# New duration estimates for the scheduler that orders one encoder block's instructions

## The chip, the cores and the metric

The kernel runs on one core of a Trainium2 chip. Its engines are TensorE (PE; PEld is its loading of stationary operands), VectorE (DVE), ScalarE (ACT), GpSimd (POOL) and SyncE (SP, which here only issues transfers). Each engine takes its instructions strictly in the order in which the program holds them. The metric is the device time of one execution in microseconds, less being better.

## The reference

One layer of a streaming encoder, 512 tokens of width 1024, float32:

```python
mod = silu(c) @ w_ada + b_ada                   # six vectors of 1024
h   = rms(x, norm1_g) * (1 + sc1) + sh1
z   = h @ w_in                                   # split by columns into
rec = hgrn2(rq, rf, ri, rg)                      # 4 heads of a gated linear recurrence
att = dsa_attention(aq, ak, av, iq, ik, iw)      # 8 heads, 256 (or 128) keys chosen per row by an index score
x   = x + g1 * (concat(rec, att) @ w_out)
h2  = rms(x, norm2_g) * (1 + sc2) + sh2
x   = x + g2 * moe(h2)                           # 16 experts, two per token inside one of four groups
```

## The kernel before

All matrix products of float32 data are made from halves: a high part rounded to fp32r (`wh`, the high half of `hx` or `mix`) and the rest (`wl`), three products per pair. ScalarE rounds the high part, VectorE subtracts it to get the low one.

The work up to the experts is written as generators, one for a piece of work, that run under a small list scheduler, `Desk`, while the program is being built. Each instruction that a generator emits goes through `Engine.call`, which estimates its duration (`cost`) and books it on its engine; `Desk.run` always steps the generator that could start first by these estimates, with a rank as tie-break inside windows of 100 ns. So the table of estimates decides nothing but the order of the instructions on each engine, and, through `either`, whether some subtractions stand on VectorE or on GpSimd (POOL). The order of the expert loop is written out by hand.

The pieces of work that matter below:

- `norm1_gen` turns eight chunks of `w_ada` into the scale and shift of the first norm: a product `a<-chunk,cB`, a copy `row`, a product `a<-sel,row`, then VectorE's `gs` and `xt` and `hx_gen`, which makes the operand `hx[k]`.
- `z_gen` makes the 33 pieces of the input projection, 24 products each (`z<-hx,wh` and `z<-hx,wl`). The first four pieces run side by side (banks z, z, o and u) and take each `hx[k]` as it comes; the fourth is `u<-hx,wB`.
- `score_gen` and `topk_gen` are the index scores and the choice of the keys, `hgrn_gen`, `level_gen` and `end_gen` the recurrence. Its subtractions `dd<-b` (seven per head) go to VectorE or POOL by `either`.
- `attend_gen(j)`, `pair_gen` and `unit_gen` are attention for the j-th of four pairs of heads, in four blocks of rows. The bias of a pair, `Wb`, comes by a transfer that POOL issues; the last two blocks add a mask to it on POOL (`nl<-Wb,negm`). A unit is: bias sum on VectorE (`nl<-a,Wb`), exponential on ScalarE, transposition on PE, a copy (`PT`), and the product `u<-PT,vv`.
- `ada_gen` is the rest of `mod`: eight groups of eight steps on VectorE (`acc<-dd,cT`), each on a transfer of 256 KB; a group ends in products on PE (`a<-acc,ones` and `a<-cs,vc`), a copy on ScalarE and a transfer that POOL issues (`modD<-acc`).
- `out_gen` is the output projection (`z<-wh,mix`), its first half on the heads of the recurrence, its second on attention's.

What POOL issues stands in POOL's one order too: a transfer behind `modD<-acc` waits until that group's copy is done.

Of the kernel before, what the change touches and what calls it, by code (L numbers as in the profile page):

```python
# [9 lines left out]
F32 = mybir.dt.float32  # L10
F32R = mybir.dt.float32r
# [6 lines left out]
PSUM = bass.MemoryType.PSUM  # L18
DRAM = bass.MemoryType.DRAM

T, D, P = 512, 1024, 128
# [143 lines left out]
class Engine:  # L165
# [5 lines left out]
    def __getattr__(self, op):  # L171
        f = getattr(self.eng, op)
        if "dma" in op or op.startswith("preload"):
            return f

        def call(*a, **k):
            r = f(*a, **k)  # L177
            o = k["out"] if "out" in k else a[0]
            n = int(np.prod(o.shape[1:]))
            port = self.name == "pool"  # L180
            if self.name == "dve" and getattr(o, "space", None) != PSUM:
                ins = [x for x in [*a[1:], k.get("in0"), k.get("in1")]
                       if hasattr(x, "shape") and int(np.prod(x.shape[1:])) > 1 and getattr(x, "space", None) != PSUM]
                port = len(ins) > 1 or op in ("tensor_copy", "tensor_scalar") and len(ins) == 1
            if self.name == "pe":
                w = a[1]
                if op == "transpose":
                    cost = 107.0
                elif w.dtype == BF16:
                    cost = max(0.4167 * n, 28.0)  # L190
                elif o.shape[0] == 32:
                    cost = 0.4167 * n
                else:
                    cost = max(0.4167 * n * (4 if w.dtype == F32 else 1), 213.0 * w.shape[0] * o.shape[0] / P ** 2)
                    if w.dtype == F32R and w.shape[0] == 64:
                        cost /= 2
            else:
                rate = self.RATE[self.name]
                if op in ("max", "activation") or op.startswith("reduce"):
                    n = int(np.prod(a[1].shape[1:])) + 100 * ("accum_out" in k)  # L200
                if op.startswith("tensor_scalar") or op in ("memset", "tensor_copy"):
                    src = a[1] if op != "memset" else None
                    if self.name == "pool" or src is None or getattr(src, "space", None) != PSUM:
                        rate *= 0.52
                cost = 60 + n * rate
            self.desk.issue(self.name, cost, port)
            return r

        return call
# [1492 lines left out]
```

## Time and profile before

| | us |
|---|---|
| median of 3 runs (lowest, highest) | 728.02 (727.63, 729.42) |
| the profiled execution | 727.48 |
| its span, first to last instruction | 725.6 |

The span is 1.9 us shorter than the execution that holds it. Of the span, PE is busy 94%, VectorE 87%, ScalarE 61%, POOL 28%. A busy PE counts every matmul from its start to a modelled end, so gaps of a few tenths of a microsecond between products do not show there. The work under the scheduler takes the span's first 412 us or so, the expert loop the rest.

### The profile page before, as it was taken

Reading aid. Unit: us, or ns where it says so; the run is one execution under the profiler, and the core shown is the slowest. Engines: PE = TensorE matmul, PEld = TensorE weight load, DVE = VectorE, ACT = ScalarE, POOL = GpSimd, SP = SyncE. Lnnn points to the kernel's source line nnn. Section 1 sums busy time; section 2 is a strip of 40 time slices with the busy share of each in tenths; the row PEclk is TensorE's granted clock in tenths of the full one; section 3 lists DMA queues with packets and bytes.
Section 4 is the critical chain, followed back from the end, with each engine's and each line's share of the span. In section 5 each row is a group of like instructions: output and inputs, shape, how many; then the busy total and the mean of one; then the engine's idle time right before and its main releaser. Section 6 shows DMA issues by size and latency. Waiting matters only on the chain.

```text
span 725.6 us, 10941 instructions
## 1 busy us (share of the span) xinstructions
PE 683.1 (94%) x3794; PEld 530.9 (73%) x3794; DVE 630.9 (87%) x1057; ACT 439.0 (61%) x670; POOL 202.4 (28%) x104
## 2 busy tenths in 40 slices
PE   3999999999999999999889979999999999999993
PEld 1666778877778776667568858888888888888872
DVE  4637889999999987978866889999999999999991
ACT  4326664545557466553343458888777777777770
POOL 0120010001321321122200030165655655556412
PEclk9999999999999999999989999999999999999997
DMA  9947532231120324685697889999999999999502
GB/s 363 406 154 224 190 111 88 89 115 59 56 90 30 117 88 164 225 308 181 188 362 305 315 318 406 390 376 347 365 363 367 354 350 358 364 361 349 187 11 33
DMA packets 57388, 172.84 MB, mean 238 GB/s; under 512 B 11954, under 2 KB 12530, under 8 KB 56304
## 3 DMA queue, kind: packets, MB, share of 16 engines
q1 hardware_dynamic: 45168, 150.54, 56.1%
q0 software_dynamic: 10720, 17.24, 8.5%
q10 hardware_dynamic: 1440, 4.31, 1.5%
q8 instruction: 32, 0.52, 0.3%
q14 instruction: 28, 0.23, 0.1%
HBM read 167.50 MB, written 15.24 MB: 252 GB/s over the span
## 4 chain that ended last, share of the span: by engine, by line
PE 50%; DMA 21%; DVE 14%; issue 10%; ACT 3%; SPq 0%; POOL 0%; POOLq 0%; DVEq 0%; ACTq 0%
PE z L177 30%; PE a L177 14%; DMA w<-in_w_dram 13%; DVE wl L177 8%; DMA out_dram<-yo,idx 6%; PE u L177 2%; PE h L177 2%; PE o L177 2%; DMA dd<-in_w_ada_dram 1%; DMA chunk<-in_w_ada_dram 1%; DVE yo L177 1%; DVE xl L177 1%; DVE oh L177 1%; ACT wh L177 1%; ACT sq L177 1%
## 5 line engine op out<-in xcount | busy, mean ns | idle before, releaser
L177 ACT CAST wh<-w 128x1024 fp32r<-128x1024 f32 x168 | 174.5, 1054 | 44.2 <-PE h L177 30.9
L177 DVE TENSOR_TENSOR wl<-w,wh 128x1024 fp32r<-128x1024 f32 x168 | 196.6, 1216 | 2.4 <-ACT wh L177 2.0
L177 PE MATMUL z<-hx,wh 128*128 128x512 f32 x496 | 163.1, 409 | 1.1 <-DVE hx L177 0.6
L1358 POOL DMA_INDIRECT out_dram<-yo,idx x16 | 123.7, 7730 | 120.8 <-DVE wl L177 64.1
L177 PEld LDWEIGHTS z<-hx,wh 128*128 128x128 f32 x496 | 88.8, 189 | 27.1 <-issue 8.7
L177 PE MATMUL h<-wl,xh 128*128 128x512 f32 x256 | 101.4, 396 | 0.0
L177 PE MATMUL h<-wh,xh 128*128 128x512 f32 x256 | 100.8, 394 | 0.0
L177 PE MATMUL h<-wh,xl 128*128 128x512 f32 x256 | 100.6, 393 | 0.0
L177 ACT CAST wh<-raw 128x1024 fp32r<-128x1024 f32 x64 | 67.1, 1052 | 55.3 <-PE z L177 48.0
L177 PE MATMUL z<-hx,wl 128*128 128x512 f32 x248 | 97.6, 394 | 0.0
L177 DVE TENSOR_TENSOR wl<-raw,wh 128x1024 fp32r<-128x1024 f32 x64 | 81.6, 1286 | 6.8 <-ACT wh L177 6.5
L177 PEld LDWEIGHTS h<-wl,xh 128*128 128x128 f32 x256 | 48.5, 189 | 12.9 <-DVE wl L177 3.0
L177 PEld LDWEIGHTS h<-wh,xh 128*128 128x128 f32 x256 | 48.5, 189 | 10.2
L177 PEld LDWEIGHTS h<-wh,xl 128*128 128x128 f32 x256 | 48.4, 189 | 10.1 <-DVE xl L177 0.3
L177 PE MATMUL y<-wh,hh 128*128 128x512 f32 x128 | 53.0, 414 | 2.0 <-DVE yo L177 2.0
L177 PEld LDWEIGHTS z<-hx,wl 128*128 128x128 f32 x248 | 46.8, 189 | 10.3
L177 PE MATMUL y<-wl,hh 128*128 128x512 f32 x128 | 50.6, 396 | 0.0
L177 PE MATMUL y<-wh,hl 128*128 128x512 f32 x128 | 50.6, 395 | 0.0
L177 PE MATMUL z<-wh,mix 128*128 128x512 f32 x128 | 48.3, 421 | 0.0
L177 DVE SCALAR_TENSOR_TENSOR acc<-dd,cT,acc 128x512 f32<-128x512 f32 x56 | 43.8, 782 | 3.6 <-DMA dd<-in_w_ada_dram 3.0
L177 POOL TENSOR_TENSOR dd<-b 128x512 f32<-128x512 f32 (+1 forms) x14 | 17.2, 1242 | 93.5 <-PE a L177 79.0
L1353 POOL DMA_INDIRECT xe<-h2D,idx x15 | 17.1, 1140 | 80.5 <-DVE idx L177 46.3
(290 smaller groups left out, 1145.2 us busy)
## 6 DMA issues: line engine op xcount, KB each, us to landing
w<-in_w_dram SPq DMA_DIRECT2D x164, 512.0 KB
raw<-in_w_in_dram SPq DMA_DIRECT2D x33, 512.0 KB
dd<-in_w_ada_dram SPq DMA_DIRECT2D x64, 256.0 KB
raw<-in_w_dram SPq DMA_DIRECT2D x24, 512.0 KB
chunk<-in_w_ada_dram SPq DMA_DIRECT2D x8, 1024.0 KB
raw<-in_w_out_dram SPq DMA_DIRECT2D x8, 512.0 KB
lineR<-lineD POOLq DMA_DIRECT2D x4, 640.0 KB, 17.6
xt<-in_xT_dram SPq DMA_DIRECT2D x4, 512.0 KB
```

What stands on the lines that cost most here:

```text
L177: r = f(*a, **k)
L1353: pool.indirect_dma_start(out=dst, out_offset=None, in_=h2D, in_offset=bass.IndirectOffsetOnAxis(ap=ix, axis=0), bounds_check=T - 1, oob_i ...
L1358: pool.indirect_dma_start(out=out, out_offset=bass.IndirectOffsetOnAxis(ap=ix, axis=0), in_=y, in_offset=None, bounds_check=T - 1, oob_is_ ...
```

## The change

The formulas of `cost` get other numbers. On PE a float32 transposition goes from 107 to 110 ns, the fp32r product of 512 columns from 213 to 231 ns, the 32-row products get a base of 60 ns, float32 products 1.95 ns a column. ScalarE's instructions become 50 ns dearer when they read PSUM and 90 ns dearer otherwise, and an accumulated output counts as 220 instead of 100 elements. On VectorE and POOL, four kinds of instruction become 100 ns dearer.

```diff
                 if op == "transpose":
-                    cost = 107.0
+                    cost = 110.0
                 elif w.dtype == BF16:
-                    cost = max(0.4167 * n, 28.0)
+                    cost = max(0.4167 * n, 50.0)
                 elif o.shape[0] == 32:
-                    cost = 0.4167 * n
+                    cost = 60 + 0.3 * n
+                elif w.dtype == F32R:
+                    cost = 18 + 0.4167 * n
+                    if w.shape[0] == 64:
+                        cost = max(cost / 2, 70.0)
                 else:
-                    cost = max(0.4167 * n * (4 if w.dtype == F32 else 1), 213.0 * w.shape[0] * o.shape[0] / P ** 2)
-                    if w.dtype == F32R and w.shape[0] == 64:
-                        cost /= 2
+                    cost = max(1.95 * n, 225.0 * o.shape[0] / P)
...
-                    n = int(np.prod(a[1].shape[1:])) + 100 * ("accum_out" in k)
+                    n = int(np.prod(a[1].shape[1:])) + 220 * ("accum_out" in k)
...
                 cost = 60 + n * rate
+                if self.name == "act":
+                    cost += 50 if getattr(a[1], "space", None) == PSUM else 90
+                elif op in ("scalar_tensor_tensor", "tensor_tensor_reduce", "tensor_tensor_scan", "copy_predicated"):
+                    cost += 100
```

No instruction is added or removed; five change their engine. Four of the 14 `dd<-b` subtractions that stood on POOL and its one `mix<-sq,mix` now stand on VectorE.

What moves is shown at three places. The first is PE near the end of the first norm, from the product on the last chunk (`chunk_322` before, `chunk_319` after) on. The operands `hx_411` and `hx_442` before are `hx[6]` and `hx[7]`; after, these are `hx_403` and `hx_436`, and `hx_336` and `hx_375` are `hx[4]` and `hx[5]`. Before:

```order
L177 MATMUL a_413<-chunk_322,cB_102 32x256 x8
L177 MATMUL z_179<-hx_411,wh_165 128x512 x2
L177 MATMUL z_179<-hx_411,wl_166 128x512
L177 MATMUL z_214<-hx_411,wh_201 128x512 x2
L177 MATMUL z_214<-hx_411,wl_202 128x512
L177 MATMUL a_413<-sel4_104,row_423 128x1 x2
L177 MATMUL o_250<-hx_411,wh_233 128x512 x2
L177 MATMUL o_250<-hx_411,wl_234 128x512
L177 MATMUL u_294<-hx_411,wB_274 128x512 x2
L177 MATMUL u_294<-hx_411,wB_275 128x512
L177 MATMUL z_179<-hx_442,wh_165 128x512 x2
L177 MATMUL z_179<-hx_442,wl_166 128x512
```

And now:

```order
L177 MATMUL a_402<-chunk_319,cB_102 32x256 x8
L177 MATMUL z_179<-hx_403,wh_165 128x512 x2
L177 MATMUL z_179<-hx_403,wl_166 128x512
L177 MATMUL a_402<-sel4_104,row_417 128x1 x2
L177 MATMUL z_210<-hx_403,wh_197 128x512 x2
L177 MATMUL z_210<-hx_403,wl_198 128x512
L177 MATMUL o_254<-hx_403,wh_234 128x512 x2
L177 MATMUL o_254<-hx_403,wl_235 128x512
L177 MATMUL u_294<-hx_336,wB_274 128x512 x2
L177 MATMUL u_294<-hx_336,wB_275 128x512
L177 MATMUL u_294<-hx_375,wB_274 128x512 x2
L177 MATMUL u_294<-hx_375,wB_275 128x512
```

The fourth piece now lags two operands behind the others (three more of its products, on `hx[6]`, follow, then the products on `hx[7]`). Six products fewer stand ahead of the last chunk's product, nine fewer ahead of its `a<-sel,row`, and 15 instead of 6 between that one and the first product on `hx[7]`.

The second place is VectorE just ahead of the third pair's first bias sum (`ISA nl,nmx<-a,Wb 128x128`). Before:

```order
L177 TENSOR_SCALAR acc<-dd,cT 128x512
L177 SCALAR_TENSOR_TENSOR acc<-dd,cT,acc 128x512
L177 TENSOR_TENSOR mix<-sq,mix 128x512
L177 SCALAR_TENSOR_TENSOR acc<-dd,cT,acc 128x512
L177 TENSOR_TENSOR wl<-raw,wh 128x1024
L177 SCALAR_TENSOR_TENSOR acc<-dd,cT,acc 128x512
L177 TENSOR_TENSOR raw<-raw,g1b 128x1024
L177 SCALAR_TENSOR_TENSOR acc<-dd,cT,acc 128x512
L177 ISA nl,nmx<-a,Wb 128x128
```

And now:

```order
L177 TENSOR_SCALAR acc<-dd,cT 128x512
L177 SCALAR_TENSOR_TENSOR acc<-dd,cT,acc 128x512 x7
L177 SCALAR_TENSOR_TENSOR sq<-u,vc,sq 128x512
L177 TENSOR_TENSOR wl<-raw,wh 128x1024
L177 TENSOR_TENSOR mix<-sq,mix 128x512
L177 TENSOR_TENSOR raw<-raw,g1b 128x1024
L177 ISA nl,nmx<-a,Wb 128x128
```

The fourth group of `ada_gen` is now complete there; before, four of its eight steps were done. Over all, 16 more VectorE instructions stand ahead of this bias sum: eleven steps of `ada_gen` (ten of them SCALAR_TENSOR_TENSOR), the four subtractions and the one low half that came from POOL. On PE, six products of the projection fewer and two groups' closing products more stand ahead of the transposition that follows it. On POOL the order there is this, before:

```order
L177 TENSOR_TENSOR dd<-b 128x512 x4
L177 TENSOR_TENSOR nl<-Wb,negm 128x384 x2
L177 TENSOR_TENSOR nl<-Wb,negm 128x512 x2
L177 TENSOR_TENSOR mix<-sq,mix 128x512
L1029 DMA modD<-acc 4x128
L945 DMA Wb<-lineR 128x2x512
L177 TENSOR_TENSOR nl<-Wb,negm 128x384
```

And now:

```order
L177 TENSOR_TENSOR dd<-b 128x512 x3
L951 DMA Wb<-lineR 128x2x512
L177 TENSOR_TENSOR nl<-Wb,negm 128x384 x2
L1035 DMA modD<-acc 4x128
L177 TENSOR_TENSOR nl<-Wb,negm 128x512 x2
L1035 DMA modD<-acc 4x128
L951 DMA Wb<-lineR 128x2x512
L1035 DMA modD<-acc 4x128
L177 TENSOR_TENSOR nl<-Wb,negm 128x384 x2
```

The last `Wb` of each piece is the third pair's. It stood behind the third group's `modD` and now stands behind the fourth group's. The four subtractions in a row, all of the last head, are gone from POOL; the three that now stand in a row are of two heads.

The third place is PE at the end of attention, from the fourth pair's norm (`a<-sq,csm`) on. Before, both halves of the last group's closing products stand behind it (the eight rows of them are cut to two):

```order
L177 MATMUL a<-sq,csm 128x512
L177 MATMUL a<-d_3474,csm 128x512
...
L177 MATMUL a<-acc,ones 32x128
L177 MATMUL a<-cs,vc 32x128
L177 MATMUL z<-wh,mix 128x512
L177 MATMUL z<-wl,mix 128x512
L177 MATMUL z<-wh,mix 128x512 x2
L177 MATMUL z<-wl,mix 128x512
L177 MATMUL z<-wh,mix 128x512
L177 MATMUL a<-cs,sh2b 128x128 x4
L177 MATMUL z<-wh,mix 128x512
```

And now:

```order
L177 MATMUL a<-sq,csm 128x512
L177 MATMUL a<-d_3495,csm 128x512
L177 MATMUL z<-wh,mix 128x512
L177 MATMUL z<-wl,mix 128x512
L177 MATMUL z<-wh,mix 128x512 x2
L177 MATMUL z<-wl,mix 128x512
L177 MATMUL z<-wh,mix 128x512 x2
L177 MATMUL z<-wl,mix 128x512
L177 MATMUL z<-wh,mix 128x512
L177 MATMUL a<-cs,sh2b 128x128 x4
L177 MATMUL z<-wh,mix 128x512
```

The last group's closing products now stand ahead of the norm, with the last steps of `ada_gen` on VectorE ahead of the fourth pair's last copy; three of VectorE's `ada_gen` steps that stood between the fourth pair's last scaling and the low half of the next norm's scale are gone from there. Behind the last row shown the order is the same but for swaps of single instructions, and from the expert loop on it is the same altogether.

## Rows read from the trace of the kernel before

**Rows 1.** Busy time by stretch: length; PE, PEld, DVE, ACT, POOL; granted clock; DMA.

```profile
100.00:171.50 71.50, 71.01 (x347) 57.79 (x346) 70.05 (x176) 35.97 (x56) 4.28 (x3) 1.00 0.24 78
171.50:295.20 123.70, 122.26 (x832) 94.33 (x831) 113.50 (x232) 74.91 (x163) 27.83 (x25) 1.00 0.30 99
...
366.00:412.00 46.00, 44.71 (x282) 38.13 (x280) 31.70 (x79) 19.95 (x43) 1.16 (x2) 0.97 0.85 330
...
440.00:680.00 240.00, 240.00 (x1167) 195.06 (x1166) 239.72 (x277) 190.78 (x212) 127.98 (x26) 1.00 0.99 363
```

**Rows 2.** The chain of waits, one piece: start us, us, what.

```profile
110.55 16.37 PE z L177 x72
```

**Rows 3.** PE's timeline, last chunk of the first norm: start, us, instruction, [idle before].

```profile
48.28 1.07 PE L177 MATMUL a<-chunk,cB 128*32 128x256 f32 x16
...
51.34 0.50 PE L177 MATMUL a<-sel,row 128*128 128x1 f32 x4
...
53.83 0.50 PE L177 MATMUL z<-hx,wh 128*128 128x512 f32 x1 [0.49 <-ACT hx L177]
...
57.46 1.12 PE L177 MATMUL a<-zs,on 64*128 64x512 f32 x2
```

**Rows 4.** Durations by form: least/median/most ns, first and last start.

```profile
L177 DVE SCALAR_TENSOR_TENSOR acc<-dd,cT,acc x56: 723/748/1505, 73.8 to 364.0; 128x512 f32<-128x512 f32 x56
L177 DVE TENSOR_TENSOR dd<-b x14: 541/678/998, 98.5 to 266.4; 128x512 f32<-128x512 f32 x11, 128x384 f32<-128x384 f32 x3
```

**Rows 5.** What VectorE waited for from 60 to 100 us: total, times, longest.

```profile
DVE wl L177 <- ACT wh L177: 3.3, 3, 1.9
DVE score L177 <- ACT relu L177: 2.6, 2, 1.6
```

**Rows 6.** The same from 100 to 295.2 us, the three longest.

```profile
DVE PT L177 <- PE a L177: 2.7, 5, 1.0
DVE nl L177 <- PE a L177: 2.6, 2, 1.4
DVE sq L177 <- ACT sq L177: 1.5, 3, 1.1
```

**Rows 7.** Timelines of VectorE and POOL near 246 us.

```profile
246.12 4.62 DVE L177 TENSOR_TENSOR wl<-raw,wh 128x1024 fp32r<-128x1024 f32 x1
245.51 4.14 POOL L177 TENSOR_TENSOR dd<-b 128x512 f32<-128x512 f32 x4
```

**Rows 8.** Timelines of ScalarE, POOL, VectorE, PE near the third pair's first bias sum.

```profile
287.69 0.25 ACT L177 COPY acc<-a 128x128 f32<-128x128 f32 x1
288.23 0.83 POOL L1029 DMA_DIRECT2D modD<-acc  x1 [13.54 <-ACT acc L177]
289.06 0.76 POOL L945 DMA_DIRECT2D Wb<-lineR  x1
295.22 0.29 DVE L177 CUSTOM_DVE_ANT_0 nl<-a,Wb 128x128 f32<-128x128 f32 x1 [0.60 <-PE a L177]
296.53 0.38 PE L177 MATMUL a<-cs,nl 128*128 128x128 f32 x2
```

**Rows 9.** The tile Wb: from issue to landing.

```profile
DMA to landing us min/median/max: 4.0/5.3/5.7
```

**Rows 10.** Timelines of PE, ScalarE and VectorE from 360 to 371.1 us.

```profile
364.94 0.68 PE L177 MATMUL a<-acc,ones 128*32 128x128 f32 x8 [4.99 <-DVE acc L177]
365.97 0.80 PE L177 MATMUL z<-wh,mix 128*128 128x512 f32 x1
368.89 0.48 PE L177 MATMUL z<-wh,mix 128*128 128x512 f32 x1
362.11 0.62 ACT L177 CAST mix<-sq 128x512 fp32r<-128x512 f32 x1 [0.82 <-DVE sq L177]
365.84 1.22 DVE L177 TENSOR_TENSOR wl<-raw,wh 128x1024 fp32r<-128x1024 f32 x1
371.01 0.69 DVE L177 TENSOR_TENSOR xm<-xm,z 128x512 f32<-128x512 f32 x1 [2.81 <-PE z L177]
```

## Prediction

> **What bounds the kernel now.** I read the chain of waits first, then the busy time by stretch, then each engine's waits and timeline where the order changes. The chain is, up to 358 us, almost all PE: 72 products of one piece of the projection run in 16.37 us without a break [rows 2], 0.227 us each. In the expert loop PE and VectorE are both full, 240.00 and 239.72 of 240 us, at the full clock [rows 1]. The change leaves the loop's order as it is, so it can do nothing there but start it earlier or later.
>
> Before the loop PE is the engine whose idle time counts, and VectorE is close behind: from 100 to 295.2 us it is busy 70.05 + 113.50 = 183.6 of 195.2 us, or 94% [rows 1]. PE really stands still at two places. Near 50 us it waits for the operands of the first norm [rows 3]; from 360 to 364.94 us it waits 4.99 us for the last sum of `ada_gen` on VectorE [rows 10]. So what the new order is worth is what it takes from these two waits, less what it adds to PE's waiting in between. I call the three terms A, B and C. A microsecond gained on PE in the first norm goes through to the end if no wait behind it eats it.
>
> **A, the first norm: −2.0 us.** From the last chunk's product (48.28) to the layer norm's first product (57.46) PE takes 9.18 us. The work in it is that chunk 1.07, `a<-sel,row` 0.50 and, counted in the order before, 24 projection products, 24 × 0.227 = 5.45: together 7.02. So 2.2 us are idle [rows 2, 3]. After, the chunk has six products fewer ahead of it: 48.28 − 1.36 = 46.92. `a<-sel,row` follows at 46.92 + 1.07 + 0.68 (three products) = 48.67. From that product to the first product on `hx[7]` the chain over VectorE and ScalarE took 53.83 − 51.34 = 2.49 us, so the operand would be there at 51.2. PE has 15 products to do in the meantime: 48.67 + 0.50 + 3.41 = 52.6. It no longer waits; twelve more products, 2.72, bring the layer norm to 55.3, or 2.2 earlier. I take 2.0, as I did not follow each chain ahead of this one. Bounds: −2.2, all of the idle time, and 0, if the chunks themselves come late.
>
> **B, the middle: +3.2 us.** Ahead of the third pair's first bias sum (295.22 now) VectorE gets 16 more instructions. Eleven are steps of `ada_gen`, 11 × 0.748 = 8.2; four are `dd<-b`, 4 × 0.678 = 2.7; one is a low half of the same shape, 0.7 [rows 4]. That is 11.6 us: made up nowhere, the bias sum would come at 306.8. PE's own work ahead of it changes by nothing: six products fewer, 1.4, and two groups' closing products more, 0.68 each for the first half [rows 2, 10]. So PE would be ready for it at 295.22 − 2.0 = 293.2.
>
> VectorE can make up at most 18.1 us: A's 2.0, because its inputs come earlier; the waits for ScalarE from 60 to 100 us, 3.3 + 2.6 = 5.9 [rows 5]; the three longest waits from 100 us on, 2.7 + 2.6 + 1.5 = 6.8 [rows 6]; and one long instruction. The last is `wl<-raw,wh` at 246.12, which took 4.62 us while POOL did four `dd<-b` in 4.14 us [rows 7]; alone it takes 1.22 [rows 10], and those four subtractions are the ones that leave POOL: 3.4. An engine with more to do finds its inputs ready more often, but not always. I take all of A, of the first waits their two longest, 1.9 + 1.6 = 3.5, of the second about three quarters, 5.0, and all of the 3.4. That is 13.9, and VectorE would stand at the bias sum at 306.8 − 13.9 = 292.9: in time.
>
> Here I weigh a rule. The Trainium skill ("SBUF — State Buffer", section "SBUF: two separate sides") says that a VectorE operation with two SBUF inputs and a GpSimd operation lock each other out for a whole instruction. Rows 7 agree, 4.62 against 1.22. By that rule the four subtractions could have cost VectorE up to their whole 4.14, not 3.4, and the sum would be 0.7 lower; the row decides.
>
> But the bias sum needs the bias too. `Wb` is issued on POOL, now behind the third group's `modD` (288.23), after the change behind the fourth's. That group's last sum stands four VectorE instructions ahead of the bias sum: a step 0.75, `wl` 1.22, a low half 0.68, and `raw<-raw,g1b`, of `wl`'s size, 1.22; together 3.9 [rows 4, 10]. Then come PE's closing product 0.68 [rows 10], ScalarE's copy 0.25, the hand-over to POOL 288.23 − 287.94 = 0.3, the `modD` issue 0.83 [rows 8], and `Wb` from issue to landing 5.3 [rows 9]: 7.4. So the bias lands 7.4 − 3.9 = 3.5 us after VectorE is ready for it: 296.4. PE, ready at 293.2, loses 3.2 at the transposition that follows (296.53 before [rows 8]; there would be 297.7). Queued behind that sum on VectorE are the steps and copies of pair three; PE has its products of the pair queued behind the transposition.
>
> In general B = 17.1 − x, where x is what VectorE makes up, and never below 0. Bounds: x = 17.1 gives 0; x = 5.4, one third of the 16.1 besides A and nothing for A, gives 11.7.
>
> **C, the tail: −2.0 us.** After, the last `ada_gen` group's sum is done before the fourth pair's norm, so the wait of 4.99 us no longer has that cause. PE must then wait only for `wl` of the third output piece. `mix`'s low half follows ScalarE's high half, 362.11 + 0.62 = 362.7; low half 0.68, `gs2b` (of `wl`'s size) 1.22, then `wl` 1.22: done at 365.8, against 365.84 + 1.22 = 367.06 now [rows 4, 10]. The first two pieces fit into the wait. From the third piece's first product to the addition `xm<-xm,z` it took 371.01 − 368.89 = 2.1 us, so the addition comes at 367.9, or 3.1 earlier [rows 10]. Two things speak for less. The norm stands behind the group's closing products, some 0.4 later. And after the wait the products ran slowly, 0.80 at 365.97 and 0.48 at 368.89 [rows 10], with a granted clock of 0.97 over the next 46 us [rows 1]; with the pieces in the gap more of them may fall on the lower level. I take −2.0; bounds −3.1 and +0.5 (no gain, norm later).
>
> **The rest: 0.** From 366 to 412 us PE is busy 44.71 of 46 [rows 1] and the order stays but for swaps; the subtractions leave a POOL that is busy 4.28 of 71.50 and 27.83 of 123.70 us there, so they free nothing that anyone waits for, beyond the 3.4 above.
>
> **Sum.** −2.0 + 3.2 − 2.0 = −0.8: 727.48 becomes 726.7. The median of the runs is 0.5 above the profiled execution, so I predict 727.2. A difference under 0.3%, 2.2 us, can't be told from none.
>
> **Rivals.**
> - *VectorE decides, slower.* The place is the third pair's first bias sum. VectorE makes up one third of the 16.1 and all of A: x = 7.4, B = 9.7, time 727.48 − 4.0 + 9.7 = 733.2, or 733.7 as a median; with one half, 731. Each microsecond not made up costs one; the change breaks even at B = 4.0, x = 13.1, which is under 1 us from my choice. For it: 94% busy, and waits that other engines cause, which extra work fills only where it stands ahead of them. Against: the 3.4 are nearly sure. The Trainium skill ("Perfetto Trace Analysis", section "Identifying the Most-Contended Engine") takes the engine with the highest occupancy as the one that bounds, and judges TensorE by its weight loads. By rows 1 that is VectorE here, 94% against (57.79 + 94.33) / 195.2 = 78%, which would speak for this rival; the unbroken products in rows 2 speak against it.
> - *VectorE makes up nearly all, faster.* x reaches 17.1, `Wb` lands in time, B = 0: 723.5, as a median 724.0; with A and C at their bounds 722.7. Further waits of VectorE or of PE that I leave out of the sum could take it to 719.
> - *No effect.* The gains at A and C are eaten by the next wait (the layer norm at 57.46 is followed by PE work that VectorE feeds), B is small: 728.
>
> **Chances.** My forecast, within 2.2 us of before: 0.36; no effect: 0.04; VectorE decides: 0.29; all made up: 0.31. So faster 0.31, same 0.40, slower 0.29. The range 719 to 735 reaches over both rivals; the forecast's own is 725.8 to 730.2.
>
> **What would show it.** A: the product `a<-zs` at about 55.3. B: no `wl` near 246 us over 1.5 us; `Wb` of the third pair issued behind the fourth `modD`; PE idle about 3 us before the transposition `a<-cs,nl`, and VectorE's bias sum held by that transfer (if held by nothing, VectorE is late itself and the first rival is right). C: no wait for `acc` after the fourth norm; less time from that norm to the first `xm<-xm,z` than now. Loop: the same length in both. What would make the prediction wrong most easily is x, since I chose it between 5 and 18; next, PE work that fills the stall I put at the transposition.

## The result, and the profile after

The changed kernel takes 737.11 us (median of 4 runs, 734.48 to 739.44) against 728.02 before. The ratio is 1.0124, with a 95% interval of 1.0101 to 1.0147. It is slower by 9 us; I had forecast 727.2 and a range of 719 to 735. Its profiled execution, the slowest of the four, took 739.44 us; its span is 737.5, so 11.9 us more than the span before. Two executions further down, 1133.84 us in the fourth run and 973.93 us in the eighth, ran at a mean granted clock of 0.61 and 0.66 and stand in no median.

Where the time went is seen by laying the two traces side by side at instructions that both have. The last column is the share of the stage that ends there.

| PE or VectorE starts | before | after | later by | added in this stage |
|---|---|---|---|---|
| layer norm `a<-zs` (end of A) | 57.46 | 57.49 | 0.0 | 0.0 |
| third pair's first transposition (B) | 296.53 | 302.19 | 5.7 | +5.6 |
| fourth pair's norm `a<-sq,csm` | 357.76 | 362.55 | 4.8 | −0.9 |
| first `xm<-xm,z` of the second half (C) | 371.01 | 373.95 | 2.9 | −1.9 |
| first product of the experts `h<-wh,xh` | 414.53 | 426.64 | 12.1 | +9.2 |

The expert loop behind it is as long as before: from its first product to the last one of this kind, 284.3 us in both traces. Half of B's loss is made up by the two stages behind it. The largest loss lies in the 43.5 us (before) between the first `xm<-xm,z` and the first expert's product, the output projection's second half and the router, which I had costed at 0. I call this stage the tail.

The busy time by stretch of the changed kernel, with the columns of [rows 1], which hold the same stretches of before:

```profile
100.00:171.50 71.50, 67.90 (x326) 54.91 (x326) 71.32 (x177) 33.93 (x54) 6.34 (x5) 1.00 0.27 89
171.50:295.20 123.70, 122.25 (x833) 93.51 (x832) 116.93 (x240) 72.85 (x160) 19.91 (x19) 1.00 0.35 115
366.00:412.00 46.00, 38.82 (x205) 30.91 (x204) 26.72 (x58) 17.34 (x37) 1.11 (x5) 0.93 0.58 212
```

In the first of them PE is busy 67.90 instead of 71.01 us while VectorE is full (71.32 of 71.50). In the third, where the same work comes some 3 us later, PE has 5.9 us less of busy time, and the granted clock is 0.93 instead of 0.97. What PE waited for in the tail of the changed kernel (total us, times, longest):

```profile
PE o L177 <- ACT hT L177: 2.6, 2, 1.3
PE u L177 <- ACT hT L177: 1.3, 1, 1.3
PE z L177 <- DVE wl L177: 0.9, 2, 0.7
PE a L177 <- DVE xm L177: 0.4, 1, 0.4
```

The kernel before waited there for `wl` alone (1.2 us). The three waits for `hT`, the operand of the router's product, are new. Timelines of VectorE, ScalarE and PE of the changed kernel around the first of them:

```profile
385.49 0.69 DVE L177 TENSOR_TENSOR xm<-xm,z 128x512 f32<-128x512 f32 x1 [1.27 <-PE z L177]
386.36 0.24 DVE L177 SCALAR_TENSOR_TENSOR L<-u,ss,cb 128x20 f32<-128x20 f32 x1 [0.18 <-PE u L177]
386.77 1.27 DVE L177 SCALAR_TENSOR_TENSOR h<-h,ss,sh2b 128x1024 f32<-128x1024 f32 x1
...
386.21 0.63 ACT L177 ACTIVATE sc<-xm 128x512 f32<-128x512 f32 x1 [1.45 <-DVE xm L177]
388.08 0.34 ACTq L1296 DMA_DIRECT2D h2D<-h  x1
388.46 0.45 ACTq L1297 DMA_DIRECT2D out_dram<-xm  x1
388.95 0.59 ACT L177 COPY hT<-a 128x512 f32<-128x512 f32 x1 [2.01 <-DVE e L177]
...
386.23 0.66 PE L177 MATMUL a<-cs,xm 128*128 128x128 f32 x4
389.59 1.07 PE L177 MATMUL o<-wr,hT 128*128 128x20 f32 x8 [1.31 <-ACT hT L177]
```

And the same block in the kernel before:

```profile
382.44 0.24 DVE L177 SCALAR_TENSOR_TENSOR L<-u,ss,cb 128x20 f32<-128x20 f32 x1 [1.75 <-PE u L177]
382.86 1.28 DVE L177 SCALAR_TENSOR_TENSOR h<-h,ss,sh2b 128x1024 f32<-128x1024 f32 x1
384.05 0.68 DVE L177 TENSOR_TENSOR xm<-xm,z 128x512 f32<-128x512 f32 x1
...
384.17 0.34 ACTq L1290 DMA_DIRECT2D h2D<-h  x1
384.54 0.45 ACTq L1291 DMA_DIRECT2D out_dram<-xm  x1
385.09 0.63 ACT L177 ACTIVATE sc<-xm 128x512 f32<-128x512 f32 x1 [3.89 <-DVE gm L177]
385.72 0.57 ACT L177 COPY hT<-a 128x512 f32<-128x512 f32 x1
```

ScalarE issues the two stores of a block of rows, and the first of them must wait until VectorE has finished that block's `h`. Before, VectorE does `L` and `h` of a block and then the next block's addition `xm<-xm,z`; by the time ScalarE needs the next `hT`, the stores are out of its way. After, the addition stands ahead of `L` and `h` in three of the four blocks. PE turns the new `xm` at 386.23, ScalarE could copy it at about 386.9, but the stores stand ahead of that copy and wait for `h`, which ends at 388.0. The copy starts at 388.95, and PE waits 1.31 us, and again at 401.19 and 412.47. (The row puts the copy's wait down to VectorE's `e`; what stands just ahead of it on ScalarE is the second store, issued at 388.46 in 0.45 us, and the first run below, without the stores there, has no such wait.)

The waits for `hT` are 3.95 of the 9.2 us. The rest is, by size, mostly the clock. Busy time of the changed kernel in five pieces of the tail (columns as in [rows 1]):

```profile
374.00:390.00 16.00, 13.76 (x85) 11.29 (x84) 10.05 (x24) 6.57 (x15) 0.00 (x0) 1.00 0.69 269
390.00:396.00 6.00, 6.00 (x26) 4.62 (x26) 2.21 (x3) 1.52 (x5) 0.00 (x0) 0.72 0.26 101
396.00:412.00 16.00, 13.83 (x79) 11.11 (x77) 9.41 (x25) 5.90 (x14) 0.00 (x0) 1.00 0.36 110
412.00:422.00 10.00, 9.08 (x51) 8.70 (x52) 6.93 (x24) 3.61 (x8) 0.00 (x0) 0.66 0.98 369
422.00:426.60 4.60, 4.60 (x48) 4.58 (x47) 1.53 (x4) 1.08 (x2) 0.00 (x0) 1.00 0.79 305
```

Behind the first and the third wait the granted clock falls to half (0.50 from 416 to 420 us). Weighed by the clock, 0.28 × 6 + 0.34 × 10 = 5.1 us of full speed are missing. The kernel before has 1.00 throughout this stage.

### The profile page after: what moved, and what is told of

The parts are those of the page before. It is cut to its first block, busy times and chain, and to the rows that moved or that the text cites. A ratio compares the mean times of both kernels' runs of the same rounds, so it can differ in the third digit from the quotient of the medians.

```text
span 737.5 us, 10928 instructions
## 1 busy us (share of the span) xinstructions
PE 690.1 (94%) x3794; PEld 535.0 (73%) x3794; DVE 632.9 (86%) x1062; ACT 439.8 (60%) x670; POOL 196.1 (27%) x99
## 4 chain that ended last, share of the span: by engine, by line
PE 36%; DMA 29%; DVE 24%; issue 7%; ACT 2%; SPq 0%; ACTq 0%; POOL 0%; POOLq 0%; DVEq 0%
DMA w<-in_w_dram 22%; PE z L177 19%; PE a L177 10%; DVE wl L177 8%; DMA out_dram<-yo,idx 4%; DVE dd L177 2%; DVE m L177 2%; DMA dd<-in_w_ada_dram 2%; PE u L177 2%; PE h L177 2%; PE o L177 2%; DVE scores L177 2%; DMA chunk<-in_w_ada_dram 1%; DVE sq L177 1%; DVE atn L177 1%
## 5 line engine op out<-in xcount | busy, mean ns | idle before, releaser
L177 PE MATMUL z<-hx,wh 128*128 128x512 f32 x496 | 165.1, 414 | 1.7 <-DVE hx L177 0.9
L177 DVE TENSOR_TENSOR wl<-raw,wh 128x1024 fp32r<-128x1024 f32 x64 | 78.9, 1245 | 3.0 <-ACT wh L177 2.7
L177 POOL TENSOR_TENSOR dd<-b 128x512 f32<-128x512 f32 (+1 forms) x10 | 15.1, 1514 | 94.9 <-DVE acc L177 34.4
```

## Experiments

Theory 1: the tail's loss is ScalarE's queue, that is, `hT` behind the stores. Rival: it comes from the new order ahead of the tail, and the tail only shows it late. The first two kernels take the stores off ScalarE, in the changed kernel and, as a control, in the one before:

```diff
-        act.dma_start(h2D[t * P:(t + 1) * P, :], h2)
-        act.dma_start(out[t * P:(t + 1) * P, :], xm[t])
+        pool.dma_start(h2D[t * P:(t + 1) * P, :], h2)
+        pool.dma_start(out[t * P:(t + 1) * P, :], xm[t])
```

> The changed kernel with one edit: the two stores of each block of rows behind the experts' norm (h2D<-h and out_dram<-xm) are issued by POOL instead of ScalarE; no estimate and no other instruction moves. Theory 1 (ScalarE's queue): in the changed kernel the copy hT<-a stands on ScalarE behind these two issues, which wait for VectorE's h, and PE's product with the router waits 1.48 us for it three times (387.9, 399.5, 410.8 us), after which products run slowly for some us. Then the edit gives back at least 3 x 1.48 = 4.4 us and up to about 7 with the slow products: 737.1 becomes 730 to 733, and no wait of o<-wr,hT or u<-wr,hT for hT is left. Rival 2 (the loss lies in the order ahead of the tail, or in the first waits of the tail at 367 to 370 us): 736 to 738, the waits move to something else.

Measured: 727.26 us (725.33 to 730.47), ratio to the kernel before 0.9986 (0.9968 to 1.0004), below the 730 to 733 that I expected. No wait for `hT` is left; the tail takes 45.3 instead of 52.7 us. ScalarE in that kernel, at the same block, goes from `sc` straight to the copy:

```profile
384.53 0.63 ACT L177 ACTIVATE sc<-xm 128x512 f32<-128x512 f32 x1 [1.43 <-DVE xm L177]
...
385.25 0.59 ACT L177 COPY hT<-a 128x512 f32<-128x512 f32 x1
```

> The kernel before with the same edit, as a control. In its trace no product waits for hT, so theory 1 expects 728 within 1 us. If issuing from POOL itself is worth several us (because ScalarE has less to do, or costs VectorE its port), it shows here, above or below 728 by more than 2, and the first run must be read against it.

Measured: 726.01 us, ratio 0.9967 (0.9956 to 0.9979). The control gains 2 us, at the edge of what I allowed. They are not in the tail (43.4 us, before 43.5) but at the very end: from the first expert's product to the end of the span it takes 309.1 instead of 311.1 us, with the 284.3 us of the loop unchanged in it. Why the end comes sooner I did not settle. The profiles of the changed kernel and of the first run are 12.0 us apart: 7.4 are the tail, 1.4 the end, 2.0 the first norm, where the lower clock struck only one of them (see A below), and 1.2 the stages between. Theory 1 holds for the tail; the medians are 9.9 us apart, more than it gave, for these other reasons.

The next two split the change in time: the mark "mw" is set when attention is done, where the tail begins. The new table stands in the first branch and the old one in the second; the fourth run has the condition the other way round.

```diff
+            if "mw" not in self.desk.done:
...
+            else:
...
```

> The new estimates up to the end of attention, the old ones from there on (second half of the output projection, router). The order is that of the changed kernel ahead of that point and nearly that of the kernel before behind it. Theory 1 (the tail's order costs about 9 of the 12 us by which the profiled changed kernel is late): the first addition of the second half comes about 3 us later than before, the tail adds nothing: 730 to 732. Rival 2 (the loss comes from ahead of the tail, which only shows it late): 735 to 738.

Measured: 729.35 us, ratio 1.0004 (0.9989 to 1.0018), just below what theory 1 gave.

> The old estimates up to the end of attention, the new ones from there on. Theory 1: the whole tail loss without the head's: 728 + 6 to 9 = 734 to 737, with PE waiting for hT as in the changed kernel. Rival 2: 727 to 730, no such waits.

Measured: 738.39 us, ratio 1.0129 (1.0102 to 1.0155), the whole loss and a little above the forecast. PE waits for `hT` three times, 3.8 us in all. The rival is out: the head of the change costs nothing that can be told (its interval reaches to 1.3 us), its tail everything.

Which of the new numbers do it? Used alone in the tail, PE's, ScalarE's or VectorE's change the position of no addition `xm<-xm,z` against `L`; PE's and ScalarE's together move two. The fifth run uses these two groups in the tail, with this condition for the new table; the sixth has PE, VectorE and POOL in it:

```diff
+            if "mw" in self.desk.done and self.name in ("pe", "act"):
```

> The old estimates up to the end of attention; from there on PE's and ScalarE's new ones, VectorE's and POOL's stay old. In the order made by it, VectorE's addition xm<-xm,z of the next block stands ahead of L and h of this block for two of three blocks (three with all the new estimates in the tail, none in the kernel before). Theory 1 (each such swap makes ScalarE's hT wait behind the stores, some 2.2 us of PE's time each, 6.6 us for three in the profiled fourth run): 728 + 2 x 2.2 = 732.4, two waits of about 1.45 us for hT. Rival (the tail's loss is of another kind, spread over the order): 734 to 738, or 728.

Measured: 732.34 us, ratio 1.0052 (1.0037 to 1.0068), with two waits for `hT`, 1.3 and 1.2 us. That it meets the forecast so closely is luck: the 2.2 us a swap came from a trace with a fall of the clock in the tail, while this trace has 1.00 there, a tail 3.5 us longer than before, and is 2.3 us late already where the tail begins.

> The same with PE's, VectorE's and POOL's new estimates in the tail and ScalarE's old. No block has the addition ahead of L; in one it stands between L and h. Theory 1: 727 to 730, at most one short wait for hT. Rival (any new order in the tail costs): 732 to 738.

Measured: 734.56 us, ratio 1.0089 (1.0063 to 1.0115). Here theory 1 missed in size. There is one wait for `hT`, in the last block, of 1.0 us, and it is dear, because the clock falls behind it:

```profile
405.00:416.00 11.00, 9.52 (x54) 8.58 (x53) 6.80 (x23) 4.89 (x10) 0.00 (x0) 0.69 1.00 367
416.00:420.50 4.50, 4.50 (x47) 4.48 (x46) 1.53 (x3) 0.59 (x1) 0.00 (x0) 1.00 0.82 318
```

0.31 × 11 = 3.4 us are missing there; with the wait, 0.5 for `xm` and 1.4 us that it is late already at the second addition, that is about the 6.0 by which this trace enters the loop late. So the number of swaps is not the price: by these traces a wait costs itself, 1.0 to 1.3 us, and what the clock does behind it.

Term B remains: in the head PE is 5.6 us late by the third pair, where I had 3.2. Its waits of 100 to 171.5 us, in the changed kernel:

```profile
PE a L177 <- DVE dd L177: 2.8, 2, 1.5
PE z L177 <- DVE qg L177: 0.8, 2, 0.4
```

The kernel before has 0.5 us there, none of it for VectorE. To see whether VectorE's load makes these waits, the seventh and eighth run lighten it and keep the order, in the changed kernel and in the control (both leave out most columns in three rounds of the choice of keys):

```diff
+            w = 32 if r in (2, 3, 4) else NB[b]
-            dve.max(m8[:, b - 1], score[b])
+            dve.eng.max(m8[:, b - 1], score[b][:, 0:w])
+            desk.issue("dve", 60 + NB[b] * 1.04, False)
...
-            dve.match_replace(score[b], m8[:, b - 1], score[b], MARK)
+            dve.eng.match_replace(score[b][:, 0:w], m8[:, b - 1], score[b][:, 0:w], MARK)
+            desk.issue("dve", 60 + NB[b] * 1.04, True)
```

> The changed kernel with the stores on POOL, and with rounds 3 to 5 of the 16 of the choice of keys cut to 32 columns on VectorE (left out of the computation: the rest of the columns in these rounds), the order of all instructions being kept. It frees VectorE of some 8 us before 165 us. Theory (what I called B: between 120 and 168 us PE waits four times, 0.54 + 0.54 + 1.5 + 1.7 = 4.3 us, because VectorE, busy 71.3 of 71.5 us, is late with qg and dd): these waits go, 727.3 - 4.3 = 723 within 1. Rival (PE waits there for ScalarE's exponentials, or its order is at fault and VectorE's load is not): 726 to 728, the waits stay.

Measured: 725.15 us, 2.1 below the first run (I had expected 4.3; by the rows above the four waits are 3.6). Three of the four waits are gone, one is left:

```profile
PE a L177 <- DVE dd L177: 1.3, 1, 1.3
```

From the layer norm to the third pair's transposition it takes 241.5 us, 3.1 less than in the first run (244.6).

The wait that is left is the last of the four. Shortly ahead of the `dd` that ends it, VectorE has a `wl` that took 2.06 us beside POOL's `dd<-b`, here and in the changed kernel; in the changed kernel:

```profile
165.99 2.06 DVE L177 TENSOR_TENSOR wl<-raw,wh 128x1024 fp32r<-128x1024 f32 x1
163.63 3.34 POOL L177 TENSOR_TENSOR dd<-b 128x512 f32<-128x512 f32 x2 [34.44 <-DVE acc L177]
```

That is 0.8 us more than the 1.22 of [rows 10], as at 246 us before [rows 7], and now in the stretch where VectorE is full. How much of the last wait comes from it no run separates.

> The kernel before with the stores on POOL and the same rounds cut. Its PE has no such waits between 100 and 171 us, so by the theory only little can be won: 726.0 - 0 to 1.5 = 724.5 to 726. If it wins as much as the changed kernel does, VectorE's load costs both alike and the theory of B falls.

Measured: 727.54 us, ratio 0.9993 (0.9975 to 1.0011); the same distance is 239.5 us, as without the cut (239.4). So VectorE's load makes waits in the new order that the old order does not have. The time lies 1.5 us above the second run and outside what I expected; where that comes from is not shown.

Last, all with the stores on POOL, one group of numbers alone in the whole program (ninth run PE, as here, tenth ScalarE, eleventh VectorE and POOL), and in the twelfth one number of the new table corrected:

```diff
+            if self.name == "pe":
...
-                    cost = 18 + 0.4167 * n
+                    cost = 14 + 0.4167 * n
```

> Only PE's new estimates, everywhere, with the stores on POOL. Its order has both gains of the changed kernel: more products ahead of the first one on the last operand of the first norm (A), and the last group of ada_gen ahead of the fourth pair's norm (C). Theory: PE's numbers also make B (they let PE's recurrence products stand earlier than VectorE can feed them): PE waits of 3 us or more for VectorE's dd and qg between 100 and 171 us, and the time is that of the changed kernel with the stores on POOL, 726 to 728. Rival: B comes with VectorE's or ScalarE's numbers; then no such waits and 721 to 724.

Measured: 740.97 us, ratio 1.0186 (1.0133 to 1.0239).

> Only ScalarE's new estimates, with the stores on POOL. Its order too has the last group of ada_gen ahead of the fourth pair's norm (C) and nine instead of six products ahead of the last operand (most of A). Theory: no B waits, so 726.0 - 2.3 - 1 to 2 = 722 to 723. Rival: B is made by ScalarE's numbers: 726 to 728 with waits of 3 us between 100 and 171 us.

Measured: 739.70 us, ratio 1.0158 (1.0127 to 1.0189).

> Only VectorE's and POOL's new estimates, with the stores on POOL. Its order has neither A nor C (the last group of ada_gen stays behind the fourth pair's norm). Theory: 725 to 728, like the kernel before with the stores on POOL, no waits of 3 us between 100 and 171 us. Rival (B is made by these numbers): 729 to 731.

Measured: 736.40 us, ratio 1.0117 (1.0082 to 1.0153).

> The changed kernel with the stores on POOL and one number set to what the chain of waits shows: an fp32r product of 512 columns 227 instead of 231 ns. A and C stay in its order. Theory: with PE's estimate 2% too long the scheduler takes PE for later than it is and lets it run ahead of VectorE, so the right number removes part of the waits between 100 and 171 us: 724 to 726. Rival: such a small number only reshuffles the order, the waits move or stay: 726 to 730.

Measured: 727.39 us, ratio 0.9982 (0.9961 to 1.0002), as without the edit.

The times of the first three went against me: with one group alone the kernel is 8 to 13 us slower than before, though the stores hold nothing up any more. PE's longest waits, from 57 to 420 us, are for VectorE in all three; for the ninth, tenth and eleventh run, in this order:

```profile
PE a L177 <- DVE dd L177: 7.7, 8, 2.5
```

```profile
PE o L177 <- DVE atn L177: 3.3, 1, 3.3
PE a L177 <- DVE acc L177: 2.6, 3, 1.8
```

```profile
PE a L177 <- DVE dd L177: 7.3, 3, 3.8
PE z L177 <- DVE wl L177: 3.0, 2, 2.8
```

From the layer norm to the first expert's product these three take 372.1, 367.1 and 367.5 us, the second run 356.4; PE is idle there for 21.3, 13.7 and 15.9 us, in the second run for 9.3. In the tenth and eleventh the clock falls there too (0.57 from 207 to 215 us, 0.53 from 201 to 212 us), so waits alone are not the whole of it.

The waits of B, for `dd` and `qg` from 100 to 171.5 us, did come as expected: none in the tenth and eleventh run, and in the ninth 4.0 us, against 3.6 in the changed kernel:

```profile
PE a L177 <- DVE dd L177: 2.5, 2, 1.7
PE z L177 <- DVE qg L177: 1.5, 1, 1.5
```

So PE's numbers make waits of this kind by themselves, the other groups' do not; that the changed kernel's come from them is likely, but the orders differ, and no run takes PE's numbers alone out of it. The corrected number of the twelfth run takes these waits from 3.6 to 1.7 us, and the way to the third pair's transposition is 242.1 instead of 244.6 us; behind it the way to the first expert's product is 2.2 us longer, and the time stays.

## Why the prediction was wrong

**What bounds the kernel.** Right as far as it goes: the loop stayed as long as it was (283.2 to 285.2 us in all runs), and what moved its start was what PE lost ahead of it. But that is idle time and granted clock together, not idle time alone, and the end behind the loop moved too, by about 2 us, with the stores.

**A, −2.0: right in size, not seen in the one profile.** The operand waits of [rows 3] are gone in the changed kernel, and yet `a<-zs` came at 57.49. The chunks did not hold it: PE waited for a transfer only at the first chunk. Its first products ran slowly for longer. The granted clock from 24 to 29 us, in the changed kernel and in the first run, and the last chunk in the first run:

```profile
24.00:29.00 5.00, 5.00 (x21) 3.42 (x23) 3.10 (x6) 1.69 (x3) 0.00 (x0) 0.50 1.03 366
24.00:29.00 5.00, 5.00 (x35) 3.52 (x34) 3.61 (x6) 2.65 (x5) 0.25 (x1) 1.00 1.03 371
```

```profile
46.94 1.07 PE L177 MATMUL a<-chunk,cB 128*32 128x256 f32 x16
55.46 1.12 PE L177 MATMUL a<-zs,on 64*128 64x512 f32 x2
```

With 1.00 there, the first run meets the forecast nearly to the digit, 46.92 and 55.3. Profiles that were slow for about as long are to be compared: the first and the seventh run have 55.46 and 54.89, the kernel before and the fourth to sixth and eighth run, with the old order, 57.10 to 57.80; the second run, with the old order and 0.52 from 24 to 29 us, has 59.76 against the 57.49. Either way it is 2.3 us. (The third run, slow for part of the time, has 56.08; the twelfth, slow until 28 us, 58.08; the ninth to eleventh have orders of their own.) Whether the new order makes the slow start longer, these few profiles can't tell.

**B, +3.2: sign right, place and cause wrong.** It measured 5.6 (244.70 from the layer norm to the transposition, before 239.07), and each of its steps failed. In the changed kernel:

```profile
287.26 0.74 DVE L177 SCALAR_TENSOR_TENSOR acc<-dd,cT,acc 128x512 f32<-128x512 f32 x1
291.23 0.77 POOL L951 DMA_DIRECT2D Wb<-lineR  x1
296.61 0.75 DVE L177 SCALAR_TENSOR_TENSOR acc<-dd,cT,acc 128x512 f32<-128x512 f32 x1 [0.75 <-DMA dd<-in_w_ada_dram]
300.88 0.29 DVE L177 CUSTOM_DVE_ANT_0 nl<-a,Wb 128x128 f32<-128x128 f32 x1
302.19 0.27 PE L177 MATMUL a<-cs,nl 128*128 128x128 f32 x1
```

- The chain over `Wb` that I made the price did not hold anything: its issue came at 291.23, 4.7 us to landing (the median of the four), so 295.9, and the bias sum at 300.88 was not waiting for it. I had misread the order. The group of `ada_gen` that is complete just ahead of the bias sum is the fifth, not the fourth, with its last step at 296.61 (in the kernel before, five steps of the fourth are done there, not four). The fourth's last step, on which this `Wb` hangs, came at 287.26.
- VectorE made up x = 306.8 − 300.88 = 5.9 us, in the first run, which has A's gain, 306.8 − 298.78 = 8.0, and not the 13.9 I took.
- By my formula x = 5.9 would have cost 11.2. It did not, as PE was not waiting for the bias sum either: no idle time stands ahead of 302.19.

Of the 5.6, 3.4 are idle time of PE (5.4 us against 1.9 from the layer norm to the transposition), and most of that fell 130 to 180 us earlier, in the stretch where VectorE is full, with PE's products on `qg` and `dd` put ahead of what VectorE could deliver. Where the other 2.2 went is open. I looked for VectorE's lateness only at the first instruction where ada_gen's extra work was all in, not in the stretch of [rows 1] where there is no idle time to make it up in. The stretched `wl` at 246 us is gone, as I had said; the one at 165.99 is new.

**C, −2.0: right.** From the fourth norm to the first `xm<-xm,z` it took 13.25 us before and 11.40 after; the wait for `acc` there is gone. Besides the wait for `wl` that I had left PE, there is one for ScalarE's `wh`:

```profile
368.55 0.50 PE L177 MATMUL z<-wh,mix 128*128 128x512 f32 x1 [1.22 <-ACT wh L177]
370.60 0.79 PE L177 MATMUL z<-wl,mix 128*128 128x512 f32 x1 [1.55 <-DVE wl L177]
```

And my fear that more pieces would fall on the lower level came true: the granted clock is 0.57 from 370 to 374 us, and in the first run 0.51 over the first 5.2 us of the tail, which there is 45.3 us long, in the second run 43.4.

**The rest, 0: the step that failed.** I wrote that from 366 to 412 us "the order stays but for swaps" and gave these no price. These swaps, in three blocks VectorE's addition ahead of `L` and `h`, put ScalarE's copy `hT` behind two stores that wait for `h`: +9.2 us in the profile, 4 of waits and about 5 of clock. With it repaired (first run) the change is worth about what the sum without it comes to, A −2.3, B +5.6, the stretch from there to `xm` −2.7: +0.6; the first run is 1.25 us above its control, and the third has a ratio of 1.0004. That the gains at A and C and the loss at B cancel is near my sum of −0.8 in size only, since B is another thing than I had priced. The scheduler could not see it: `Engine.__getattr__` hands transfers through without a cost, so a store on ScalarE's queue waits in no estimate.

**The rivals.** The outcome has the sign of the first one, but not its place. The sign that I had named for it is there, a bias sum held by nothing; but PE did not wait for that sum, and with the old tail the new head is no slower (1.0004), so what VectorE does not make up is not what decided. None of my rivals had the tail.

## What to carry to other kernels

When an order changes, go through each engine's queue for instructions that wait for another engine (a transfer's issue above all) and ask what newly stands behind them; a swap of single instructions is free only if the one that now comes second had nothing waiting behind it. A scheduler's table of costs is worth what the whole of it is worth: here one engine's new durations without the others' made the kernel 8 to 13 us slower, and all of them together changed it by about 1 us once the queue was mended. If the scheduler leaves a class of instructions out of its model, its better estimates elsewhere can put work behind just these. The version that beats both is the old order with the stores on POOL, 0.9967 of before (0.9956 to 0.9979): a small gain, but clear of its interval.

## What the hardware showed that I had not expected

- A wait of PE of 1.0 to 1.3 us was followed by the lower clock in some cases and not in others: granted clock 0.66 over the 10 us that begin with the wait at 412 us, 1.00 over the 16 us with the wait at 401 us, in the same execution. In the fourth run, with the same tail order, the profiled execution kept 1.00 behind its last wait and took 734.8 us; the others took 734.5 and 738.3 to 739.4. Their mean granted clock is 0.984 in the two short ones and 0.975 to 0.978 in the long ones, so one more fall of the clock costs, as an estimate from these, some 4 us.
- How long the first products run slowly differs between executions: in the kernel before they took full speed at about 24 us, in the changed kernel, in its one profile, at 29 us, which cost it some 2 us.
- Moving two stores of each block from ScalarE to POOL shortened the end of the program, 300 us later, by 1.4 to 2 us. What holds it there stays open.
